# Gate and up of 18 feed-forward tiles as a 2x2 block product with seven block products instead of eight

## The chip, the cores and the metric

The kernel runs on one core of a Trainium2 chip, as one launch. The metric is the device time of that core in microseconds. Three runs of the kernel before gave 1388.51, 1388.89 and 1391.63 us; the median is 1388.89 us. TensorE does the matrix products (PE in the profile, PEld its weight loads), VectorE (DVE) and ScalarE (ACT) the element-wise work, GpSimd (POOL) a little more of it and some DMA issues, and SyncE (SP) issues most DMAs.

## The reference

Two layers of a recurrent decoder. Each has a mixer and a SwiGLU feed-forward, both modulated by shift, scale and gate vectors computed from a condition, and both followed by a layer norm. 512 prompt tokens and 8 sample tokens go through the same weights. What the change touches:

```python
D_MODEL = 1024; DEPTH = 2; D_FF = 2816      # D_FF: 22 tiles of 128 columns

def swiglu(h, w_in, w_out):
    gate, up = jnp.split(jnp.einsum('bld,df->blf', h, w_in), 2, axis=-1)
    return jnp.einsum('blf,fd->bld', jax.nn.silu(gate) * up, w_out)

for l in range(DEPTH):
    mod = jnp.einsum('bd,de->be', silu(c), w_ada[l]) + b_ada[l]      # 6 x D_MODEL columns
    sh_m, sc_m, gt_m, sh_f, sc_f, gt_f = jnp.split(mod, 6, axis=-1)
    out = mixer_l(x * (1 + sc_m) + sh_m)                             # even, then odd (S5 and HGRN2)
    x = layer_norm(ALPHA * x + (1 + gt_m) * out, ln_g[l, 0], ln_b[l, 0])
    h = x * (1 + sc_f) + sh_f
    x = layer_norm(ALPHA * x + (1 + gt_f) * swiglu(h, ffn_w_in[l], ffn_w_out[l]), ln_g[l, 1], ln_b[l, 1])
```

All inputs are float32.

## The kernel before

Activations lie features on partitions, tokens along the free axis: 8 blocks (`k`) of 128 features, and 520 tokens as two halves (`hf`) of `HN` = 260. An activation is kept as two float32r parts, `hhi` and `hlo` (the rounded value and the rest), and so is each weight (`whi`, `wlo`); a product is the three matmuls hi·hi, lo·hi and hi·lo. So one tile of 128 output columns is 8 blocks x 2 halves x 3 = 48 matmuls of 128x128 weights and 260 columns. This is `mm3` (lines 231 to 241).

Weights come through `WS` (lines 152 to 226), a stream in the order of the list `plan`. `load` issues one DMA into one of three `raw` tiles; `make` turns 128 columns of it into a pair: `S.copy` on ACT rounds to `whi` (L199), `sub` on DVE leaves the rest in `wlo` (L110). Three such pairs exist (pool `whl`), used in turn. `take` makes the pair of this unit and of the next at raised priority. Where `first_units` runs, two pairs go to another pool, tag `W` (`wxh`, `wxl`).

`ffn` (from line 835) does the 22 tiles of gate and up in two halves of 11, with the down projection of each half behind it. Gate goes to SiLU (ACT), up is multiplied with it (DVE, L110 `sg<-acc,sg`), and the product is split into `ah` (ACT) and `al` (DVE). PSUM has two `acc` tiles of two banks and four `mx` tiles of one bank. At the start of a feed-forward `first_units` does the first five units (a unit is gate or up of one tile) for the first token half and then for the second, because the layer norm delivers the halves one after the other. The last feed-forward (`l` = 1) is the last stage of the kernel.

The modulation vectors (`ada`) are matmuls with 32 columns of weights, four side by side in the array, over chunks of 1 MB that are mixed into `plan`: 10 blocks of 1024 outputs, 4 chunks each (L323). In the S5 preparation, 32 groups get a small 128x16 product each (`pM`, L1620), done while the first feed-forward runs.

The order of instructions on each engine is fixed when the program is built, by a scheduler that goes by data dependences, buffers and priorities; on the chip each engine takes its queue in that order and waits at semaphores.

Of the kernel before, what the change touches and what calls it, by code (L numbers as in the profile page):

```python
# [34 lines left out]
FIRST = 3000  # L35
EV_COLS = [256, 1552, 512, 1808, 768, 1024, 1280, 2064, 2320]
# [3 lines left out]
def build(tc, I, O):  # L40
    nc = tc.nc
    V, S, G, T, SY = nc.vector, nc.scalar, nc.gpsimd, nc.tensor, nc.sync
    with ExitStack() as ctx:
# [107 lines left out]

        class WS:
# [29 lines left out]
            def make(self, u):  # L182
# [6 lines left out]
                if kind in ("ada", "lr"):  # L189
                    self.prep[u] = r  # L190
                    return
                m = min(128, ncol)
# [8 lines left out]
                self.prep[u] = (hi, lo)  # L201

# [10 lines left out]
            def ada(self):  # L213
                while self.i < len(units) and plan[units[self.i][0]][0] == "ada":
# [4 lines left out]
                    if p_[2] == 6:  # L219
                        ada_rows(self.acc, p_[6], p_[4] // 128)  # L220
# [27 lines left out]
        def p_ada(l, js):  # L248
            return [("ada", I["w_ada"][l], k0, 2, D * j, D, l) for j in js for k0 in range(0, 8, 2)]
# [4 lines left out]
        def p_ffn(l, hb):  # L254
            r = []
            for c in range(0, 11, 2):
                n = min(2, 11 - c) * 128
                c0 = (11 * hb + c) * 128
                r.append(("fin", f_in[l], 0, 8, c0, n))
# [16 lines left out]

        FA = p_ada(0, [5]) + p_ada(1, [0])
        FB = p_ada(1, [1, 2])
        OA = p_ada(1, [3, 4])
        LA = p_ada(1, [5])  # L280
        plan.append(("lr", ev_in, 0, 8, 1536, 16))
        plan += p_cols("in", ev_in, [0])
        plan += mix(p_cols("in", ev_in, EV_COLS), p_ada(0, range(2, 4)))
        plan += mix(p_cols("out", ev_out, (0, 256)), p_ada(0, [4])[:2], 1) + p_ada(0, [4])[2:] + p_cols("out", ev_out, (512, 768))
# [5 lines left out]
        plan += mix(p_ffn(1, 0)[:12], LA, 2, 1) + p_ffn(1, 0)[12:] + p_ffn(1, 1)  # L290
# [18 lines left out]
        def ada_mm(p, r):  # L309
# [4 lines left out]
            sb = cst.tile([128, 256], F32, tag="adasb", name="adasb")  # L314
# [5 lines left out]
        def ada_part(p, k0, r):  # L320
            for k in range(2):
                for c in range(4):
                    T.matmul(p[32 * c:32 * c + 32, 0:256], condT[:, k0 + k, :], r[:, k, 256 * c:256 * c + 256],  # L323
                             start=(k0 + k == 0), stop=(k0 + k == 7), tile_position=(0, 32 * c), skip_group_check=True)

        def ada_rows(p, l, j):
            sb = cst.tile([128, 256], F32, tag="adasb", name="adasb")
            S.copy(sb, p[:, 0:256])
            for b in range(2):
                transpose(p[:, 256 + 128 * b:384 + 128 * b], sb[:, 128 * b:128 * b + 128])  # L330
# [1687 lines left out]
```

## Time and profile before

| | |
|---|---|
| median of three runs | 1388.89 us |
| profiled execution, its own time | 1391.37 us |
| span of the profile | 1389.4 us |
| PE busy in the span | 1333.4 us, 96% |
| DVE, ACT, POOL busy | 55%, 36%, 14% |
| mean granted TensorE clock | 0.985 of full speed |
| last feed-forward | about 994 to 1389 us of the span |

The profile is one execution. Times in its rows are microseconds from the start of the span unless they are marked ns. PE's busy time counts the time in which a matmul is under way; since matmuls are pipelined, one lasts longer than the distance to the next. Busy shares are averages over stages with different limits, so a stage is read by its own rows.

### The profile page before, as it was taken

How to read it: one execution, taken by the hardware profiler on the slowest of the kernel's cores; microseconds unless marked ns; L12 is line 12 of the kernel's file. 1: busy time of each engine (PE TensorE's matmuls, PEld its weight loads, DVE VectorE, ACT ScalarE, POOL GpSimd, SP SyncE). 2: the span in 40 equal slices, each digit the busy share in tenths (PEclk: the TensorE clock that was granted, in tenths of full speed). 3: DMA queues.
4: the chain of work that ended last, by engine and by line, in shares of the span. 5: the costliest groups of instructions: out<-in, count | busy, mean ns of one | idle time of the engine just before them, and what ended most of it. 6: DMA issues, size and time to landing. Idle time of an engine off the chain costs nothing. (4 is left out here: it accounts for less than half of the span.)

```text
span 1389.4 us, 29467 instructions
## 1 busy us (share of the span) xinstructions
PE 1333.4 (96%) x12687; PEld 1267.0 (91%) x12687; DVE 764.9 (55%) x1726; ACT 498.2 (36%) x802; POOL 191.8 (14%) x215
## 2 busy tenths in 40 slices
PE   6998999989999999999998999999999999999996
PEld 4797988989998999999988999889899999999996
DVE  4677755687997233233592785566833233232365
ACT  3555536353232222222264123363533222222231
POOL 2200010340011200000170421013500000000013
PEclk9999999999999999999999999999999999999998
DMA  9643363413345842444458446432333323221211
GB/s 277 197 152 101 91 212 120 154 48 120 116 166 205 234 152 92 152 133 158 150 200 169 131 147 216 126 126 92 101 113 107 118 95 122 92 92 54 84 62 63
DMA packets 157628, 185.53 MB, mean 134 GB/s; under 512 B 18188, under 2 KB 137354, under 8 KB 157242
## 3 DMA queue, kind: packets, MB, share of 16 engines
q1 hardware_dynamic: 151514, 166.43, 38.7%
q0 software_dynamic: 5744, 17.08, 3.8%
q8 instruction: 100, 1.64, 0.5%
q14 instruction: 30, 0.25, 0.1%
q10 hardware_dynamic: 240, 0.13, 0.0%
HBM read 167.11 MB, written 15.36 MB: 131 GB/s over the span
## 5 line engine op out<-in xcount | busy, mean ns | idle before, releaser
L237 PE MATMUL acc<-hhi,whi 128*128 128x260 f32 x1936 | 398.8, 287 | 3.0 <-ACT whi L199 1.3
L199 ACT CAST whi<-raw 128x1024 fp32r<-128x1024 f32 (+2 forms) x198 | 187.7, 955 | 587.1 <-PE acc L239 428.1
L239 PE MATMUL acc<-hlo,whi 128*128 128x260 f32 x1936 | 396.2, 286 | 1.2 <-DVE hlo L110 1.2
L241 PE MATMUL acc<-hhi,wlo 128*128 128x260 f32 x1936 | 395.1, 285 | 0.0
L110 DVE TENSOR_TENSOR wlo<-raw,whi 128x1024 fp32r<-128x1024 f32 (+2 forms) x198 | 220.2, 1116 | 222.3 <-ACT whi L199 220.7
L237 PEld LDWEIGHTS acc<-hhi,whi 128*128 128x128 f32 x1936 | 300.5, 190 | 16.1 <-issue 5.9
L239 PEld LDWEIGHTS acc<-hlo,whi 128*128 128x128 f32 x1936 | 300.6, 190 | 4.4 <-DVE hlo L110 1.7
L241 PEld LDWEIGHTS acc<-hhi,wlo 128*128 128x128 f32 x1936 | 300.9, 190 | 2.3 <-issue 1.7
L239 PE MATMUL acc<-al,whi 128*128 128x260 f32 x576 | 116.0, 283 | 2.3 <-DVE al L110 2.3
L237 PE MATMUL acc<-ah,whi 128*128 128x260 f32 x576 | 116.4, 284 | 1.4 <-DVE x L122 0.8
L241 PE MATMUL acc<-ah,wlo 128*128 128x260 f32 x576 | 115.7, 283 | 0.0
L110 DVE TENSOR_TENSOR sg<-acc,sg 128x520 f32<-128x520 f32 (+1 forms) x48 | 31.0, 653 | 112.6 <-PE acc L241 108.1
L237 PEld LDWEIGHTS acc<-ah,whi 128*128 128x128 f32 x576 | 88.3, 188 | 4.8 <-ACT whi L199 2.3
L239 PEld LDWEIGHTS acc<-al,whi 128*128 128x128 f32 x576 | 88.6, 188 | 2.5 <-DVE al L110 2.5
L241 PEld LDWEIGHTS acc<-ah,wlo 128*128 128x128 f32 x576 | 88.6, 188 | 0.0
L524 POOL TENSOR_TENSOR s<-x 128x520 f32<-128x520 f32 x4 | 6.9, 1720 | 568.1 <-ACT whi L199 321.6
L110 DVE TENSOR_TENSOR smp<-acc,gt 128x8 f32<-128x8 f32 (+1 forms) x72 | 11.6, 161 | 119.0 <-PE acc L241 94.5
L816 PE MATMUL acc<-hhi,whi 128*128 128x260 f32 x208 | 59.2, 287 | 3.3 <-ACT hhi L774 3.3
L818 PE MATMUL acc<-hlo,whi 128*128 128x260 f32 x208 | 58.8, 289 | 3.3 <-DVE hlo L767 1.9
L817 PE MATMUL acc<-hhi,wlo 128*128 128x260 f32 x208 | 58.3, 282 | 0.0
L122 DVE SCALAR_TENSOR_TENSOR x<-acc,gt,x 128x512 f32<-128x512 f32 (+1 forms) x72 | 44.8, 622 | 0.0
L323 PE MATMUL mx<-raw,condT 128*32 128x256 f32 x640 | 44.2, 384 | 0.0
(592 smaller groups left out, 2017.5 us busy)
## 6 DMA issues: line engine op xcount, KB each, us to landing
raw<-in_w_ada_dram SPq DMA_DIRECT2D x40, 1024.0 KB, 6.1
raw<-in_ffn_w_in_dram SPq DMA_DIRECT2D x40, 1024.0 KB, 5.2
raw<-in_ffn_w_out_dram SPq DMA_DIRECT2D x16, 1024.0 KB, 5.3
raw<-in_ev_w_in_dram SPq DMA_DIRECT2D x10, 1024.0 KB, 9.4
raw<-in_od_w_in_dram SPq DMA_DIRECT2D x10, 1024.0 KB, 5.9
raw<-in_w_ada_dram SPq DMA_DIRECT2D x16, 512.0 KB, 7.3
raw<-in_ffn_w_out_dram SPq DMA_DIRECT2D x16, 384.0 KB, 3.1
raw<-in_ev_w_out_dram SPq DMA_DIRECT2D x4, 1024.0 KB, 5.3
```

The source lines that it names most:

```text
L110: V.tensor_tensor(out=out, in0=a, in1=b, op=op)
L122: V.scalar_tensor_tensor(out=out, in0=a, scalar=s, in1=b, op0=op0, op1=op1)
L199: S.copy(hi[:, :nk, :m], rj)
L237: T.matmul(acc[:, hf, :HN], wh[:, k - koff, :], ah(k)[:, hf, :], start=st, stop=False)
L239: T.matmul(acc[:, hf, :HN], wh[:, k - koff, :], al(k)[:, hf, :], start=False, stop=False)
L241: T.matmul(acc[:, hf, :HN], wl[:, k - koff, :], ah(k)[:, hf, :], start=False, stop=sp)
L323: T.matmul(p[32 * c:32 * c + 32, 0:256], condT[:, k0 + k, :], r[:, k, 256 * c:256 * c + 256], start=(k0 + k == 0), stop=(k0 + k == 7), til ...
L524: G.tensor_tensor(out=lnt["s1"], in0=x[:, 0] if m == 1 else lnt["s1"], in1=x[:, m], op=ALU.add)
L816: T.matmul(out, wh[:, k, :], ah(k)[:, hf, :], start=n == 0, stop=False)
L817: T.matmul(out, wl[:, k, :], ah(k)[:, hf, :], start=False, stop=False)
L818: T.matmul(out, wh[:, k, :], al(k)[:, hf, :], start=False, stop=n == len(ks) - 1)
```

## The change

Seen per tile f, gate and up form a 2x2 block matrix: rows gate and up, columns the lower and the upper four feature blocks. The activation forms another: rows the lower and the upper four feature blocks, columns the two token halves. The kernel before computes the eight block products. The changed one computes seven, by a scheme with sums of blocks ahead of and behind the products (each block product is 4 feature blocks x 3 = 12 matmuls). It does so for tiles 4 to 21 of the last feed-forward. Tiles 0 to 3 stay as they were.

`t_forms` makes the sums of activation blocks once, on DVE and ACT: `t1`, `t2`, `t4`, and `t3` in place of a block of `hhi`/`hlo` that is no longer needed. `sw_weights` makes four pairs per tile, in four steps: w1 (both gate blocks), w2 (one up block), wu and wg (two sums each, formed in place in `raw`). `sw_unit` runs the seven products, and forms the sums behind them by copies and additions in PSUM.

Beside that: the modulation matmuls take 512 columns at a time instead of 256 (half as many instructions, 5 blocks of 2048 outputs), and the four chunks that lay in the last feed-forward move to the first layer's input projection. The small S5 product swaps its operands: `CS` (32 columns of two groups) becomes the weights, four side by side, and two transposes per 8 groups put the result back. The pool of the final layer norm's tiles opens behind the tiles of `t_forms`. Some small tiles change place.

```diff
+SW0 = 4
+        def sw_weights(r, w, walloc):
+            g, u = r[:, 0], r[:, 1]
+
+            def parts(t, src, hs):
+                for q in hs:
+                    S.copy(t[0][:, q], src[:, q])
+                    sub(t[1][:, q], src[:, q], t[0][:, q].bitcast(F32))
+
+            def pair():
+                return tuple(whl.tile([128, 8, 128], F32R, tag=nm, name=nm) for nm in ("whi", "wlo"))
+
+            w.append(pair())
+            parts(w[0], g, (LO, UP))
+            yield
+            w.append(pair())
+            parts(w[1], u, (UP,))
+            add(u[:, UP], u[:, LO], u[:, UP])
+            sub(u[:, LO], g[:, LO], u[:, LO])
+            sub(g[:, LO], u[:, UP], g[:, LO])
+            sub(g[:, UP], g[:, UP], g[:, LO])
+            yield
+            w.append(walloc())
+            parts(w[2], u, (UP, LO))
+            yield
+            w.append(walloc())
+            parts(w[3], g, (LO, UP))
...
+                if kind == "sw":
+                    w = self.prep[u] = []
+                    self.gen = sw_weights(r, w, self.walloc)
+                    for _ in range(1 if plan[units[u - 1][0]][0] == "sw" else 4):
+                        next(self.gen, None)
+                    return
...
-            return [("ada", I["w_ada"][l], k0, 2, D * j, D, l) for j in js for k0 in range(0, 8, 2)]
+            return [("ada", I["w_ada"][l], k, 1, D * j, 2 * D, l) for j in js for k in range(8)]
...
-        plan += mix(p_ffn(1, 0)[:12], LA, 2, 1) + p_ffn(1, 0)[12:] + p_ffn(1, 1)
+        plan += p_ffn(1, 0) + p_ffn(1, 1)
...
-                             start=(k0 + k == 0), stop=(k0 + k == 7), tile_position=(0, 32 * c), skip_group_check=True)
+                T.matmul(p[32 * c:32 * c + 32, 0:512], condT[:, k, :], r[:, 0, 512 * c:512 * c + 512],
+                         start=(k == 0), stop=(k == 7), tile_position=(0, 32 * c), skip_group_check=True)
...
+                    for lo, up in qs:
+                        q1, q2, q3 = t2k("q1"), t2k("q2"), t2k("q3")
+                        join(q3, lo, 1)
+                        join(q1, lo, 0)
+                        sub(q1, q3, q1)
+                        parts(t1, lo, q1)
+                        join(q2, up, 1)
+                        sub(q2, q2, q1)
+                        parts(t2, lo, q2)
+                        join(q3, up, 0)
+                        sub(q3, q3, q2)
+                        parts(t4, lo, q3)
+                    for lo, up in qs:
+                        q2, q3 = t2k("q2"), t2k("q3")
+                        join(q3, lo, 1)
+                        join(q2, up, 1)
+                        sub(q2, q2, q3)
+                        parts(t3, lo, q2)
...
+                def sw_unit(f):
+                    w1, w2, wu, wg = ws.get("sw", 128 * f)
+                    t1, t2, t3, t4, b11, b21, b22 = tf
+                    o1, o2, e = acc_tile(), acc_tile(), mx()[:, :HN]
+                    a_, d_, c_, b_ = o1[:, 0, :HN], o1[:, 1, :HN], o2[:, 0, :HN], o2[:, 1, :HN]
+
+                    def prod(out, w, off, t, st):
+                        for k in range(4):
+                            T.matmul(out, w[0][:, off + k], t[0][:, k], start=st and k == 0, stop=False, skip_group_check=True)
+                            T.matmul(out, w[1][:, off + k], t[0][:, k], start=False, stop=False, skip_group_check=True)
+                            T.matmul(out, w[0][:, off + k], t[1][:, k], start=False, stop=k == 3, skip_group_check=True)
+
+                    soon = lambda: tc.high_priority(offset=HIGH)
+                    prod(a_, w1, 0, b11, True)
+                    with soon():
+                        S.copy(b_, a_)
+                    prod(e, wu, 4, t1, True)
+                    p5 = t2k("p5")[:, 0]
+                    with soon():
+                        S.copy(p5, e)
+                    prod(b_, wg, 0, t2, False)
+                    with soon():
+                        add(d_, b_, p5)
+                    prod(a_, w1, 4, b21, False)
+                    ws.more()
+                    prod(b_, wu, 0, t3, False)
+                    ws.more()
+                    with soon():
+                        S.copy(c_, b_)
+                    prod(d_, wg, 4, b22, False)
+                    ws.more()
+                    prod(c_, w2, 4, t4, False)
+                    with soon():
+                        add(b_, b_, p5)
+                    m = f % 11
+                    fin_ev(0, m, 0, o1[:, :, :HN])
+                    fin_ev(1, m, 0, o2[:, :, :HN])
...
-                        T.matmul(pM[:, g * 16:(g + 1) * 16], BA[:, g].rearrange("p e h -> p (e h)"), CS[:, gg],
-                                 start=True, stop=True)
+                        T.matmul(pM[32 * c:32 * c + 32, 128 * (g // 4):128 * (g // 4) + 128],
+                                 CS[:, gg:gg + 2].rearrange("p a b -> p (a b)"), BA[:, g].rearrange("p e h -> p (e h)"),
+                                 start=g < 4, stop=True, tile_position=(0, 32 * c), skip_group_check=True)
```

The order on VectorE in the last feed-forward, in the kernel before, over two tiles (`wlo` is a weight's rest, `sg` the product with the gate, `al` its rest):

```order
L110 TENSOR_TENSOR al_11640<-sg_12408,ah_11639 128x520
L110 TENSOR_TENSOR sg_12464<-acc_12529,sg_12464 128x520
L110 TENSOR_TENSOR wlo_12692<-raw_12585,whi_12691 128x1024
L110 TENSOR_TENSOR al_11640<-sg_12464,ah_11639 128x520
L110 TENSOR_TENSOR wlo_12706<-raw_12585,whi_12705 128x1024
L110 TENSOR_TENSOR wlo_12764<-raw_12695,whi_12763 128x1024
L110 TENSOR_TENSOR sg_12636<-acc_12711,sg_12636 128x520
L110 TENSOR_TENSOR wlo_12874<-raw_12819,whi_12873 128x1024
```

The same engine in the changed kernel, over one tile (7) in the first half; raw_12205 holds the weights of tile 8, raw_12333 those of tile 9. `acc_12336<-acc_12337,p5` is the sum behind product 3, `wlo_12392` is w2, `wxl_12412` is wu, `wlo_12456` is w1, `wxl_12431` is wg:

```order
L111 TENSOR_TENSOR acc_12336<-acc_12337,p5_12364 128x260
L111 TENSOR_TENSOR wlo_12392<-raw_12205,whi_12391 128x512
L111 TENSOR_TENSOR raw_12205<-raw_12205 128x512 x2
L111 TENSOR_TENSOR wxl_12412<-raw_12205,wxh_12411 128x512
L111 TENSOR_TENSOR raw_12205<-raw_12205 128x512
L111 TENSOR_TENSOR acc_12337<-acc_12337,p5_12364 128x260
L111 TENSOR_TENSOR raw_12205<-raw_12205 128x512
L111 TENSOR_TENSOR sg_12449<-acc_12337,sg_12449 128x520
L111 TENSOR_TENSOR wxl_12412<-raw_12205,wxh_12411 128x512
L111 TENSOR_TENSOR wlo_12456<-raw_12333,whi_12455 128x512 x2
L111 TENSOR_TENSOR wxl_12431<-raw_12205,wxh_12430 128x512 x2
L111 TENSOR_TENSOR al_11528<-sg_12449,ah_11527 128x520
```

Where one tile had 2 rests of 1024 columns, one product and one split, it now has 7 rests and 4 sums of 512 columns, 2 sums of 260, one product and one split: 15 instructions. wg, which product 3 of tile 8 reads, stands behind all but the last of them.

VectorE in the changed kernel where tile 4, the first of the new form, begins; `sg_11876` is the product of the last old unit, raw_11553 holds tile 4's weights, `q1`, `q2`, `q3` are sums of activation blocks, `t1l` is the second half of t1's rest, and `wlo_12072` is w1 of tile 5:

```order
L111 TENSOR_TENSOR sg_11876<-acc_11964,sg_11876 128x520
L111 TENSOR_TENSOR q3_12058<-hhi_85,hlo_86 128x520
L111 TENSOR_TENSOR wxl_11953<-raw_11553,wxh_11952 128x512
L111 TENSOR_TENSOR wlo_12072<-raw_11883,whi_12071 128x512 x2
L111 TENSOR_TENSOR q2_12057<-hhi_85,hlo_86 128x520
L111 TENSOR_TENSOR q2_12042<-q2_12042,q1_12041 128x520
L111 TENSOR_TENSOR q3_12043<-hhi_85,hlo_86 128x520
L111 TENSOR_TENSOR raw_11553<-raw_11553 128x512
L111 TENSOR_TENSOR t1l_12020<-q1_12041,t1h_12019 128x520
L111 TENSOR_TENSOR wxl_11953<-raw_11553,wxh_11952 128x512
L111 TENSOR_TENSOR al_11528<-sg_11876,ah_11527 128x520
L111 TENSOR_TENSOR q2_12057<-q2_12057,q3_12058 128x520
```

`t1l`, which product 2 of tile 4 reads, stands nine instructions behind the product of the last old unit, and the sums that belong to t2, t3 and t4 are still to come.

## Rows read from the trace of the kernel before

**Rows 1.** The page, part 1: busy us (share of the span) xinstructions.
```profile
PE 1333.4 (96%) x12687; PEld 1267.0 (91%) x12687; DVE 764.9 (55%) x1726; ACT 498.2 (36%) x802; POOL 191.8 (14%) x215
```
**Rows 2.** Busy time by stretches: length, then PE, PEld, DVE, ACT, POOL, PEclk, DMA, GB/s.
```profile
392.00:440.00 48.00, 45.15 (x396) 43.67 (x394) 40.80 (x42) 14.25 (x24) 5.95 (x9) 1.00 0.55 189
...
1052.00:1166.00 114.00, 114.00 (x971) 111.98 (x971) 37.25 (x56) 30.86 (x42) 0.00 (x0) 1.00 0.34 109
1166.00:1260.00 94.00, 94.00 (x785) 94.00 (x784) 30.39 (x35) 24.47 (x31) 0.00 (x0) 1.00 0.30 96
```
**Rows 3.** VectorE in order of time, last feed-forward: start, duration, [idle before <-releaser].
```profile
1263.16 0.70 DVE L110 TENSOR_TENSOR sg<-acc,sg 128x520 f32<-128x520 f32 x1 [3.65 <-PE acc L241]
...
1268.93 0.70 DVE L110 TENSOR_TENSOR sg<-acc,sg 128x520 f32<-128x520 f32 x1 [3.08 <-PE acc L241]
```
**Rows 4.** VectorE from 900 us, by shape: xcount | busy us, mean ns | idle before.
```profile
L110 DVE TENSOR_TENSOR sg<-acc,sg 128x520 f32<-128x520 f32 x20 | 14.0, 700 | 68.7 <-PE acc L241 68.7
...
L110 DVE TENSOR_TENSOR sg<-acc,sg 128x260 f32<-128x260 f32 x4 | 1.5, 420 | 2.7 <-PE acc L818 2.7
...
L110 DVE TENSOR_TENSOR wlo<-raw,whi 128x512 fp32r<-128x512 f32 x2 | 1.4, 690 | 0.0
```
**Rows 5.** VectorE in order of time, pairs that stand directly behind each other.
```profile
993.25 0.41 DVE L110 TENSOR_TENSOR x<-x,rs 128x256 f32<-128x256 f32 x1
993.58 0.41 DVE L767 TENSOR_TENSOR hlo<-h32h,hhi 128x256 fp32r<-128x256 f32 x1
...
1009.53 1.22 DVE L110 TENSOR_TENSOR wlo<-raw,whi 128x1024 fp32r<-128x1024 f32 x1
1010.66 0.76 DVE L110 TENSOR_TENSOR al<-sg,ah 128x260 fp32r<-128x260 f32 x2
```
**Rows 6.** ScalarE from 900 us, by shape.
```profile
L78 ACT ACTIVATE sg<-acc 128x520 f32<-128x520 f32 x19 | 11.3, 597 | 0.0
...
L741 ACT COPY mu<-mx 128x260 f32<-128x260 f32 x2 | 0.7, 370 | 0.5 <-PE mx L700 0.5
L199 ACT CAST whi<-raw 128x512 fp32r<-128x512 f32 x1 | 0.6, 617 | 4.0 <-PE acc L239 4.0
```
**Rows 7.** All engines in order of time: a weight buffer's last reader, and the cast into it.
```profile
1022.49 0.40 PE L239 MATMUL acc<-hlo,whi 128*128 128x260 f32 x2
...
1022.99 1.05 ACT L199 CAST whi<-raw 128x1024 fp32r<-128x1024 f32 x1 [3.51 <-PE acc L239]
...
1024.07 1.23 DVE L110 TENSOR_TENSOR wlo<-raw,whi 128x1024 fp32r<-128x1024 f32 x1 [0.20 <-ACT whi L199]
```
**Rows 8.** TensorE in order of time around one modulation chunk.
```profile
1051.56 0.40 PE L241 MATMUL acc<-hhi,wlo 128*128 128x260 f32 x2
1051.89 1.07 PE L323 MATMUL mx<-raw,condT 128*32 128x256 f32 x16
1052.89 0.50 PE L237 MATMUL acc<-hhi,whi 128*128 128x260 f32 x2
```
**Rows 9.** TensorE over the whole span, by line.
```profile
L323 PE MATMUL mx<-raw,condT 128*32 128x256 f32 x640 | 44.2, 384 | 0.0
...
L1620 PE MATMUL mx<-CS,BA 128*128 128x16 f32 x64 | 7.4, 257 | 0.0
...
L147 PE MATMUL mx<-ident,BA 128*128 128x128 f32 x32 | 4.1, 272 | 0.0
```
**Rows 10.** The DMA issues, the page's part 6.
```profile
raw<-in_ffn_w_in_dram SPq DMA_DIRECT2D x8, 512.0 KB, 4.1
```
**Rows 11.** TensorE in order of time: the longest wait for data in mid-kernel.
```profile
765.98 3.18 PE L1716 MATMUL mx<-u,bt 128*64 128x72 f32 x48 [5.94 <-DMA u<-Usd]
```
**Rows 12.** TensorE alone, three stretches of 3 us around it (busy, PEclk, DMA, GB/s).
```profile
764.00:767.00 3.00, 1.02 (x17) 0.61 1.09 284
767.00:770.00 3.00, 3.00 (x40) 0.50 0.53 152
770.00:773.00 3.00, 3.00 (x22) 0.75 0.19 64
```

More of the change, by code (lines that the diff above doesn't have):

```diff
@@ L174, in load @@
                     t = wraw.tile([128, 2048], F32, tag="raw", name="raw")
+                    if kind == "sw":
+                        v = t.rearrange("p (g k c) -> p g k c", g=2, k=8)
+                        for g in range(2):
+                            SY.dma_start(v[:, g], src[:, DFF * g + c0:DFF * g + c0 + 128].rearrange("(k p) c -> p k c", p=128))
+                        self.raw[self.dma] = v
+                        self.dma += 1
+                        continue
                     v = t[:, :nk * ncol].rearrange("p (k c) -> p k c", k=nk)
@@ L201, in make, with more @@
                 self.prep[u] = (hi, lo)
+            def more(self):
+                with tc.high_priority(offset=self.off):
+                    next(self.gen, None)
             def take(self):
@@ L258, in p_ffn @@
                 c0 = (11 * hb + c) * 128
+                if l and 11 * hb + c >= SW0:
+                    r += [("sw", f_in[l], 0, 8, c0 + 128 * j, 128) for j in range(n // 128)]
+                    continue
                 r.append(("fin", f_in[l], 0, 8, c0, n))
@@ L275, in mix @@
             return r
[L277 to L280, printed above, removed]
+        E2, E4 = p_ada(0, [2]), p_ada(0, [4])
+        FA, FB, OA = p_ada(1, [0]), p_ada(1, [2]), p_ada(1, [4])
         plan.append(("lr", ev_in, 0, 8, 1536, 16))
         plan += p_cols("in", ev_in, [0])
-        plan += mix(p_cols("in", ev_in, EV_COLS), p_ada(0, range(2, 4)))
-        plan += mix(p_cols("out", ev_out, (0, 256)), p_ada(0, [4])[:2], 1) + p_ada(0, [4])[2:] + p_cols("out", ev_out, (512, 768))
+        plan += mix(p_cols("in", ev_in, EV_COLS), E2 + E4[:4])
+        plan += mix(p_cols("out", ev_out, (0, 256)), E4[4:6], 1) + E4[6:] + p_cols("out", ev_out, (512, 768))
         plan += mix(p_ffn(0, 0)[:12], FA[:4], 3) + mix(p_ffn(0, 0)[12:], FA[4:])
@@ L848, in ffn @@
                     for d in range(0, 11, 2):
+                        if l and f0 + d >= SW0:
+                            break
                         nj = min(2, 11 - d)
@@ L882, in ffn @@
                             next(side, None)
+                    if l:
+                        if hb == 0:
+                            with tc.high_priority(offset=200):
+                                tf[:] = t_forms()
+                        for f in range(max(SW0, f0), f0 + 11):
+                            sw_unit(f)
+                        if hb:
+                            swx.close()
                     for _ in side or ():
@@ L899, in ffn @@
                 prep = ln_prep(l, 1, (1, 0, 1)) if l == 0 else None
-                final = None if l == 0 else final_tools(fp)
+                final = None if l == 0 else final_tools(swx.enter_context(tc.tile_pool(name="fin", bufs=1, reuse_waits="tile")))
                 for m in range(4, 8):
```

61 lines of the change are left out of this document (42 added, 19 removed).

## The prediction

> **What bounds the kernel now.** First the page's busy shares: PE is busy 96% of the span, DVE 55%, ACT 36% [rows 1]. A share over the whole span hides stages, so next the stretches of the last feed-forward: PE is busy all of the time from 1052 to 1260 us at full clock, DVE for a third of it [rows 2]. The reader is to see that this stage is matmuls and nothing else, and that two thirds of VectorE stand free. Then the price of a unit: two up units in a row end 5.77 us apart [rows 3], which is 48 matmuls, so 0.1202 us each. Last the prices on VectorE and ScalarE, since the change pays there: durations by shape [rows 4, 6], and how far apart two instructions start [rows 5], because a queue moves by that distance, not by the duration.
>
> **The matmuls saved.** A tile had 2 x 48 = 96 matmuls and gets 7 x 12 = 84. Eighteen tiles save 216, times 0.1202 us: 26.0 us. A product of 12 takes 1.44 us, a tile 10.10 instead of 11.54.
>
> **What VectorE pays.** Starts lie 0.33 us apart for 256 columns and 1.13 for 1024 [rows 5]; on the line between, 0.60 us for 512, 0.34 for 260, 0.61 for 520. A tile had two rests of 1024, one product and one split: 2 x 1.13 + 2 x 0.61 = 3.5 us. It gets eleven instructions of 512, two of 260, two of 520: 6.6 + 0.68 + 1.22 = 8.5 us of the tile's 10.10. That fits as a sum. It need not fit in time, because most of these instructions can't start early, and that is where I think the gain goes.
>
> Follow the buffers. Three pairs serve w1 and w2 in turn: w2 of tile f+1 gets the pair that w1 of tile f leaves, and w1 is last read by product 4. Only then does ScalarE cast w2's block, VectorE takes its rest, and only then may the sums be formed in place in raw, for the first overwrites that block. wu and wg of tile f+1 come out of these sums, and product 3 of tile f+1 reads wg. So one chain runs from the end of product 4 of a tile to product 3 of the next:
> - the cast into a freed pair starts 0.10 us behind the modelled end of its last reader, 0.26 us behind the place where the next matmul starts [rows 7];
> - cast of 512 columns 0.62 us [rows 6], hand-over 0.03 [rows 7];
> - w2's rest 0.69 in full [rows 4] and 0.03, because the next reads what it frees;
> - two sums 1.20, a wait of about 0.17 for ScalarE's cast of wu, wu's first rest 0.60, a sum 0.60, wu's second rest 0.60, the PSUM sum 0.34, a sum 0.60, both rests of w1 for the tile behind 1.20, the product with the gate 0.61, wg's first rest in full 0.69, hand-over 0.03: 6.64.
>
> Together 0.26 + 0.65 + 0.72 + 6.64 = 8.27 us. TensorE has products 5, 6, 7, 1, 2 and one matmul in between: 5 x 1.44 + 0.12 = 7.33. So product 3 of each tile waits 0.94 us. The order is a little different in the second half (w1 ahead of the product), with the same sum. Tile 11 doesn't pay it, as its weights are made beside the down projection, nor do tile 4, which has its own bill, and tile 5, whose weights are made while tile 4 stands. Fifteen tiles pay: 14.1 us. VectorE is the engine that decides here: if its distance is a twentieth off, the chain moves by 0.33 us a tile, 5 us in all. Nearer than that the rows don't bound it, since none shows such a chain.
>
> **The start at tile 4.** The activation sums are 28 instructions of 520 columns on VectorE (12 joins, 8 differences and 8 rests; I count all as 0.61). Most stand behind instructions that wait for TensorE: the product with the gate of tile 2 waits for the second-last old unit and so can't start before 5.55 us ahead of the last one's end. From it to t1's last rest VectorE's new order has 21 instructions: -5.55 + 20 x 0.605 + 0.7 puts its end 7.3 us behind the start of tile 4. Product 2 wants it 6 matmuls in, at 1.44 + 0.72 = 2.16: a wait of 5.1. Eight more instructions (4.8 us) lead to wg's first rest, at 12.1; product 3 wants it at 7.3 + 0.72 + 0.12 = 8.1: 4.0. Seven more end t3's second half at about 16.4, which product 5 wants at 15.5: about 1.0. Together 10.1 us, once. Nothing hides it, since TensorE's queue has only tile 4 next. In the second half there is no such bill.
>
> **The small edits.** The modulation: a chunk of 16 matmuls takes 1.0 us in four rounds of four [rows 8], 40 chunks in all (640 matmuls [rows 9]). Now 8 of twice the columns in two rounds: the same columns, two changes of round fewer. From nothing to 0.1 us a chunk, 0 to 4 us; I take 1.5, since columns fill most of a round. Four chunks leave the last feed-forward, where TensorE is never idle, and enter the first input projection, where it is nearly so: 0, give or take 1. The S5 product: 64 matmuls cost 7.4 us, 0.116 each for 16 columns [rows 9]. Per 8 groups there come 16 matmuls of 128 columns, four side by side, about half of a modulation chunk [rows 8], 0.55 us, and two transposes of 0.13 [rows 9]: 0.8 instead of 1.85, 4.2 in all. In this stretch VectorE is busy 40.8 of 48 us and PE already idle 2.85 [rows 2], so some comes back as waits: 0 to 4.2, I take 3.5. A weight load of 512 KB in rows of 128 columns lands in 4.1 us [rows 10]; two per tile are 8.2 of a tile's 11 and are issued more than a tile ahead: 0. The final layer norm's tiles wait for tile 21, some 60 us ahead of use: 0.
>
> **The sum.** -26.0 + 14.1 + 10.1 - 1.5 - 3.5 = -6.8 us, on the profiled execution's 1391.4 us (span 1389.4 and 2.0 around it). That execution lies 2.5 above the median of the runs, 1388.9; from the median the sum gives 1382 us.
>
> **Rivals.** (a) VectorE keeps up: the chain is shorter than I think, by 0.6 us of its 8.27, and the start costs 8 because ScalarE and VectorE run ahead more. Then -26.0 + 15 x 0.34 + 8 - 5 = -18: 1371 us. For it: VectorE's free time [rows 2]. Against: the buffer order, which no free time shortens.
>
> (b) Slower than before: VectorE's queue moves by full durations, 0.69 for 512 [rows 4], as soon as each instruction reads what one just ahead wrote or freed. The eleven distances in the chain grow by 0.09, so product 3 waits 1.9 us; the start's 29 grow too, to 12.6. -26.0 + 15 x 1.9 + 12.6 - 5 = +10: 1399 us. It decides from a distance of 0.64 us on, where the waits eat the 26.0 and the small edits. Against it: the pairs in rows 5 are apart less than they last, by 0.08 and 0.09. [...]
>
> [...]
>
> (d) The change doesn't do what it says: its order has 84 matmuls a tile for all eighteen, so this has no chance of its own.
>
> **How the numbers follow.** The forecast has 0.5, its own range 1376 to 1389 (chain 0.6 to 1.2 us a tile, small edits 1 to 8); (a) 0.15, (b) 0.15, (c) 0.2. About 0.3%, 4.2 us, is what a measurement of this kernel can tell from no change: faster means under 1384.7, slower over 1393.1. Faster: 0.35 of the forecast's 0.5, all of (a), 0.06 of (c): 0.56. Slower: 0.14 of (b) and 0.03 of the rest: 0.17. Between: 0.27. The range for 8 in 10 takes in most of (a) and half of (b): 1368 to 1395.
>
> **What would show it.** In the profile after: 84 matmuls a tile and tiles about 11.0 us apart, with PE idle about 0.9 us ahead of product 3, released by wg's rest on VectorE (or by the copy into PSUM beside it), in fifteen tiles; VectorE over 80% busy in the tiles; about 10 us of idle PE in tile 4, in products 2 and 3; L1620's successor at under half of 7.4 us. I am wrong in the main if tiles are 10.1 us apart (then the chain isn't there) or over 11.6, if product 3 waits for something else than VectorE or ScalarE, or if tile 4 starts without a gap.

## The result and the profile after

| kernel | median, us | ratio to before, 95% interval |
|---|---|---|
| before | 1389.4 | |
| changed | 1414.2 (1412.0 to 1415.6) | 1.0175 [1.0155, 1.0195] |
| predicted | 1382 (1368 to 1395) | |

The change costs 24.8 us; the forecast was a gain of 6.8. The profiled execution took 1415.4 us, span 1413.3, mean granted clock 0.974. Three executions that were hundreds of microseconds longer than all others of their kernel (one each of `fill`, `half2_v4` and the kernel before) are left out of all medians and ratios.

The page, part 1, of the changed kernel answers [rows 1]:
```profile
PE 1323.4 (94%) x12159; PEld 1237.9 (88%) x12159; DVE 875.0 (62%) x1947; ACT 555.9 (39%) x957; POOL 192.7 (14%) x215
```
There are 528 matmuls fewer, PE's busy time is down by 10 us, and the span is up by 24. So TensorE waits. The distance of tiles is read as in [rows 3], from VectorE's products with the gate, in order of time (start, duration); there is one a block tile:
```profile
1037.09 0.69 DVE L111 TENSOR_TENSOR sg<-acc,sg 128x520 f32<-128x520 f32 x1
...
1061.42 0.69 DVE L111 TENSOR_TENSOR sg<-acc,sg 128x520 f32<-128x520 f32 x1
...
1072.27 0.69 DVE L111 TENSOR_TENSOR sg<-acc,sg 128x520 f32<-128x520 f32 x1
...
1096.93 0.69 DVE L111 TENSOR_TENSOR sg<-acc,sg 128x520 f32<-128x520 f32 x1
...
1109.30 0.69 DVE L111 TENSOR_TENSOR sg<-acc,sg 128x520 f32<-128x520 f32 x1
...
1221.34 0.69 DVE L111 TENSOR_TENSOR sg<-acc,sg 128x520 f32<-128x520 f32 x1
...
1233.36 0.69 DVE L111 TENSOR_TENSOR sg<-acc,sg 128x520 f32<-128x520 f32 x1
```
The first block tile ends 24.3 us after the last plain one, the second 10.85 us behind it. From there tiles of the first half are 12.3 to 12.4 us apart (the last 11.3), of the second half 12.02. Plain tiles were 11.54 apart, and the forecast was 11.04. What TensorE waited for from 1000 to 1360 us (engine, line, releaser: us in total, times, longest), the four longest in total:
```profile
PE acc L939 <- DVE acc L111: 10.1, 18, 0.6
PE acc L939 <- ACT acc L946: 7.6, 10, 0.8
PE acc L940 <- DVE wxl L111: 7.4, 6, 3.4
PE mx L941 <- DVE t1l L111: 3.1, 1, 3.1
```
The reader is to see the first row: a wait in every one of the 18 tiles that the prediction does not have. One tile of the first half, all engines in order of time:
```profile
1110.71 0.37 ACT L946 COPY acc<-acc 128x260 f32<-128x260 f32 x1
...
1111.71 1.28 DVE L111 TENSOR_TENSOR wxl<-raw,wxh 128x512 fp32r<-128x512 f32 x2
...
1112.45 0.39 PE L940 MATMUL acc<-t2h,wxl 128*128 128x260 f32 x1 [0.92 <-DVE wxl L111]
...
1114.15 0.44 DVE L111 TENSOR_TENSOR acc<-acc,p 128x260 f32<-128x260 f32 x1 [0.54 <-PE acc L941]
...
1114.64 0.39 PE L939 MATMUL acc<-hhi,whi 128*128 128x260 f32 x1 [0.60 <-DVE acc L111]
```
Product 3 (t2h) waits for wg's rest, as predicted, 0.92 us. Product 4 (hhi, whi) then stands still until VectorE has written `d_ = b_ + p5`. It does not read d_: it adds to a_, the other bank of the same tile. And each wait costs more than its idle time: the three starts around the first lie 1.4 us beyond the usual 0.12, the two at the second 0.87, since idle time is counted from the modelled end of a matmul and the first two matmuls behind a wait stand 0.2 us apart. In the second half the trace names another releaser of product 3, ScalarE's copy (L946), but wg's rest stands right beside it. All engines in order of time:
```profile
1221.94 1.28 DVE L111 TENSOR_TENSOR wxl<-raw,wxh 128x512 fp32r<-128x512 f32 x2
...
1222.47 0.39 PE L939 MATMUL acc<-t2h,wxh 128*128 128x260 f32 x1 [0.77 <-ACT acc L946]
```
The first of these two rests ends at about 1222.63, and the second matmul of product 3, which reads it, starts at 1222.70. The copy had ended at 1222.42.

The start, TensorE in order of time, matmuls behind a wait:
```profile
1039.04 0.39 PE L940 MATMUL mx<-t1h,wxl 128*128 128x260 f32 x1 [1.36 <-DVE wxl L111]
...
1043.29 0.58 PE L941 MATMUL mx<-t1l,wxh 128*128 128x260 f32 x1 [3.14 <-DVE t1l L111]
...
1048.15 0.58 PE L940 MATMUL acc<-t2h,wxl 128*128 128x260 f32 x1 [3.41 <-DVE wxl L111]
...
1051.54 0.59 PE L939 MATMUL acc<-hhi,whi 128*128 128x260 f32 x1 [0.64 <-DVE acc L111]
```
and stretches of 3 us (PE, PEld, DVE, ACT, POOL busy, then PEclk), as in [rows 12]:
```profile
1041.00:1044.00 3.00, 0.71 (x3) 0.71 (x4) 3.00 (x6) 1.24 (x2) 0.00 (x0) 0.50 0.00 0
...
1053.00:1056.00 3.00, 3.00 (x15) 3.00 (x15) 0.77 (x2) 0.62 (x1) 0.00 (x0) 0.50 0.85 254
1056.00:1059.00 3.00, 3.00 (x21) 3.00 (x20) 2.77 (x5) 1.42 (x4) 0.00 (x0) 0.72 0.00 0
```
Products 2 and 3 wait, as the prediction said, 7.9 us of idle time for its 9.1; the 0.64 at product 4 is the wait that it does not have, and its 1.0 at product 5 did not come. VectorE is busy without a break beside the first three (6 instructions in each 3 us until 1050 us), and the granted clock is at 0.50 of full speed from 1041 to 1056 us.

The rows that answer to [rows 9], TensorE over the whole span, by shape:
```profile
L370 PE MATMUL mx<-raw,condT 128*32 128x512 f32 x320 | 41.9, 604 | 1.9 <-DMA raw<-in_w_ada_dram 1.9
...
L1755 PE MATMUL mx<-BA,CS 128*32 128x128 f32 x64 | 2.6, 279 | 0.0
...
L148 PE MATMUL mx<-ident,mt 128*128 128x128 f32 x8 | 1.5, 271 | 0.0
```
The small edits did on TensorE about what was priced: 44.2 became 41.9, and 7.4 became 2.6 and 1.5. But L370 now waits 1.9 us for the DMA of a chunk, where the row of before has 0.0.

### The profile page after: what moved, and what is told of

It is laid out like the page before. It is cut to its first block, busy times and chain, and to the rows that moved or that the text cites. A ratio compares the mean times of both kernels' runs of the same rounds, so it can differ in the third digit from the quotient of the medians.

```text
span 1413.3 us, 28868 instructions
## 1 busy us (share of the span) xinstructions
PE 1323.4 (94%) x12159; PEld 1237.9 (88%) x12159; DVE 875.0 (62%) x1947; ACT 555.9 (39%) x957; POOL 192.7 (14%) x215
## 5 line engine op out<-in xcount | busy, mean ns | idle before, releaser
L111 DVE TENSOR_TENSOR wlo<-raw,whi 128x1024 fp32r<-128x1024 f32 (+2 forms) x216 | 212.2, 993 | 179.5 <-ACT whi L242 133.6
L242 ACT CAST whi<-raw 128x1024 fp32r<-128x1024 f32 (+2 forms) x162 | 149.9, 933 | 419.6 <-PE acc L286 284.7
L284 PE MATMUL acc<-hhi,whi 128*128 128x260 f32 x1360 | 283.4, 289 | 2.7 <-ACT whi L242 1.3
L286 PE MATMUL acc<-hlo,whi 128*128 128x260 f32 x1360 | 282.6, 288 | 0.9 <-DVE hlo L111 0.9
L288 PE MATMUL acc<-hhi,wlo 128*128 128x260 f32 x1360 | 278.3, 285 | 0.0
L284 PEld LDWEIGHTS acc<-hhi,whi 128*128 128x128 f32 x1360 | 211.6, 190 | 22.9 <-issue 9.6
L286 PEld LDWEIGHTS acc<-hlo,whi 128*128 128x128 f32 x1360 | 212.4, 190 | 5.3 <-issue 2.1
L288 PEld LDWEIGHTS acc<-hhi,wlo 128*128 128x128 f32 x1360 | 211.8, 190 | 2.0 <-issue 1.3
L111 DVE TENSOR_TENSOR smp<-acc,gt 128x8 f32<-128x8 f32 (+1 forms) x72 | 11.6, 161 | 117.6 <-PE acc L288 91.7
L863 PE MATMUL acc<-hhi,whi 128*128 128x260 f32 x208 | 59.9, 289 | 3.3 <-ACT hhi L821 3.3
L111 DVE TENSOR_TENSOR wxl<-raw,wxh 128x512 fp32r<-128x512 f32 (+1 forms) x82 | 62.1, 771 | 1.2 <-ACT wxh L242 1.0
L160 ACT CAST whi<-raw 128x512 fp32r<-128x512 f32 x54 | 31.7, 620 | 78.8 <-issue 50.7
L865 PE MATMUL acc<-hlo,whi 128*128 128x260 f32 x208 | 59.0, 291 | 3.2 <-DVE hlo L814 1.8
L864 PE MATMUL acc<-hhi,wlo 128*128 128x260 f32 x208 | 59.0, 286 | 0.0
L939 PE MATMUL acc<-hhi,whi 128*128 128x260 f32 x144 | 43.2, 300 | 10.1 <-DVE acc L111 10.1
```

Source lines behind the costliest of these rows:

```text
L111: V.tensor_tensor(out=out, in0=a, in1=b, op=op)
L160: S.copy(t[0][:, q], src[:, q])
L242: S.copy(hi[:, :nk, :m], rj)
L284: T.matmul(acc[:, hf, :HN], wh[:, k - koff, :], ah(k)[:, hf, :], start=st, stop=False)
L286: T.matmul(acc[:, hf, :HN], wh[:, k - koff, :], al(k)[:, hf, :], start=False, stop=False)
L288: T.matmul(acc[:, hf, :HN], wl[:, k - koff, :], ah(k)[:, hf, :], start=False, stop=sp)
```

## The experiments

Theory: the block product loses by three things of the order of work and of buffers, each of which can be taken away alone: the late activation sums at the start, product 4's wait for a bank that it doesn't touch, and product 3's wait. Rivals: the early edits; VectorE's load as such (a wait taken away comes back at the next product); the clock. Medians are of each run's own set, and ratios are to the runs of before on the same chip. The sets' runs of before had medians from 1389.4 to 1391.1 us, so a difference between medians of two sets is good to 1 or 2 us; the ratios are free of this.

| run | median, us | ratio, 95% interval |
|---|---|---|
| no_blocks | 1393.7 | 1.0025 [1.0013, 1.0037] |
| nb_olds5 | 1395.1 | 1.0028 [1.0011, 1.0045] |
| own_bank | 1403.8 | 1.0090 [1.0075, 1.0105] |
| p4_first | 1410.4 | 1.0152 [1.0105, 1.0199] |
| early2 | 1404.5 | 1.0097 [1.0072, 1.0122] |
| fill | 1411.7 | 1.0136 [1.0101, 1.0171] |
| v4be2 | 1392.6 | 1.0007 [0.9990, 1.0024] |
| half2_v4 | 1392.8 | 1.0018 [1.0000, 1.0037] |
| obe2 | 1389.5 | 0.9987 [0.9971, 1.0003] |
| lean | 1392.5 | 1.0014 [0.9998, 1.0030] |
| v6p | 1399.1 | 1.0063 [1.0043, 1.0084] |
| obe3 | 1371.2 | 0.9865 [0.9832, 0.9898] |

**no_blocks**
```
-SW0 = 4
+SW0 = 22      # and no activation sums
```


> The changed kernel with all 22 tiles of the last feed-forward as plain products again; the new modulation chunks, their new places and the turned S5 product stay. Theory: the loss lies in the block tiles. In the changed kernel's trace everything ahead of the last feed-forward ended 5.9 us later, of which 4 moved modulation chunks are about 4.4, and these 4.4 then leave the last feed-forward; so this run ends about 1.5 us over the kernel before, at 1391 us (1387 to 1395). Rival: the edits ahead of the last feed-forward are a loss of their own of 6 us or more; then about 1396 us or over.

1393.7 us, 2.9 over its runs of before, between the two expectations and nearer to the theory's 1.5. The block tiles thus cost 20.5 of the loss; the early edits are a small loss where I had forecast a gain of 5. TensorE's wait for a chunk (L370) is here too, 2.0 us.

**own_bank**
```
-a_, d_, c_, b_ = o1[:, 0, :HN], o1[:, 1, :HN], ...
+a_, d_, c_, b_ = o1[:, 0, :HN], e, ...
-fin_ev(0, m, 0, o1[:, :, :HN])
+fin_ev(0, m, 0, o1[:, 0:1, :HN], slice(0, 1))
+fin_ev(0, m, 0, e.unsqueeze(1), slice(1, 2))
...
```


> The changed kernel with the sum b + p5 written into the bank of product 2 and no longer into the second bank of the tile into which product 4 accumulates; the SiLU then runs in two halves. Nothing that product 4 needs comes from VectorE then. Theory: product 4 waits only because both banks belong to one tile; 0.76 us of distance for each of 17 or 18 tiles goes, 13 us, and ScalarE's extra 0.2 us a tile is beside it: 1401 us (1398 to 1404). Rival: VectorE's queue is the bound of a tile, and the wait moves on to product 5 or to the next product 3: 1414 us, within 2.

10.4 us less, and product 4's wait is gone from the list of TensorE's waits: it was for the tile, not for the data. Tiles of the second half, VectorE in order of time:
```profile
1213.56 0.69 DVE L111 TENSOR_TENSOR sg<-acc,sg 128x520 f32<-128x520 f32 x1
...
1224.88 0.69 DVE L111 TENSOR_TENSOR sg<-acc,sg 128x520 f32<-128x520 f32 x1
```
They are 11.32 apart for 12.02, so 0.7 of the wait's 0.8 went there; product 3's wait grew from 0.77 to 1.00 us of idle time. That the gain is short of 13 goes with this: product 3's waits, 11.6 us behind the first block tile in the changed kernel (7.6 for the copy, 4.0 for wg's rest), are 18.0 now and all for the copy (TensorE's waits, 1000 to 1360 us):
```profile
PE acc L939 <- ACT acc L946: 18.0, 17, 1.7
```
The change's two banks were guarded as one tile: product 4, which touches only one of them, stood still until VectorE had written the other, 18 times (10.1 us of idle time in the changed kernel), and that is what went.

**p4_first**
```
+prod(a_, w1, 4, b21, False)
 prod(b_, wg, 0, t2, False)
 with soon():
     add(d_, b_, p5)
-prod(a_, w1, 4, b21, False)
```


> The changed kernel with product 4 ahead of product 3; nothing else. Theory: product 3 has 1.47 us more until its weights are wanted, and the second weight pair comes free 1.47 us earlier, so product 3's wait (1.1 to 1.4 us a tile) goes; product 5 now stands right behind product 3 and must wait for the sum that reads its bank, 0.6 to 0.8 us a tile as product 4 did. Some 18 to 20 us less, 1395 us (1390 to 1402). Rival: VectorE's queue is the bound of a tile (9.0 us of 12.3 busy, with waits between): then the period stays at 12 us or over and the time at 1414 us, within 3.

Only some 4 us less; the intervals of the two ratios overlap, and neither expectation holds. The trace is of the slowest of its four executions (1421.2 us). The weights' wait did go behind the first block tile, and the expected wait of product 5 came, but a second that I had not expected came with it, TensorE in order of time:
```profile
1223.28 0.39 PE L939 MATMUL acc<-hhi,wxh 128*128 128x260 f32 x1 [0.53 <-DVE acc L111]
...
1231.27 0.39 PE L939 MATMUL acc<-hhi,whi 128*128 128x260 f32 x1 [0.45 <-ACT acc L946]
```
Product 4 adds to the bank that the copy of product 1 reads, and now stands too close behind. A tile of the second half takes 11.68 us. Its first block tile took 27.3 us. The waits were moved, not removed.

**early2**
```
 first_units(...)
+if l:
+    forms = t_forms()      # t1, t2, t4; yields ahead of t3
+    next(forms)
 for u in fins[n0:]:
```


> The changed kernel with the sums of the activations (t1, t2, t4) formed right behind the first five plain tiles' halves, not at the end of the plain tiles; only t3, which overwrites an operand of the plain tiles, stays where it was. Theory: the 25 us that the first block tile took (12.3 a tile later on) come from VectorE's backlog of 21 us at that place, 18 sums of the activations among it, and from the clock that fell to 0.50 behind the waits; 8 to 12 us less, 1404 us (1401 to 1408). Rival: the first tile's own weights, whose four parts are made at one go, set its waits, and the clock falls as before: at most 3 us less, 1411 to 1414 us.

9.7 us less. The last plain unit and the first block tile, VectorE in order of time:
```profile
1037.31 0.69 DVE L111 TENSOR_TENSOR sg<-acc,sg 128x520 f32<-128x520 f32 x1
...
1049.66 0.69 DVE L111 TENSOR_TENSOR sg<-acc,sg 128x520 f32<-128x520 f32 x1
```
Two stretches of 3 us in that tile (PE, PEld, DVE, ACT, POOL busy, then PEclk):
```profile
1041.00:1044.00 3.00, 2.40 (x20) 2.19 (x19) 1.05 (x3) 0.00 (x0) 0.00 (x0) 1.00 0.38 110
1044.00:1047.00 3.00, 3.00 (x27) 3.00 (x27) 1.88 (x3) 1.48 (x3) 0.00 (x0) 1.00 0.80 240
```
The tile takes 12.35 us for 24.3, like any other: the start is gone, and the clock (1.00) doesn't fall. The next tile takes 12.38 for 10.85, so of the 12 us some 10.4 stay.

**fill**
```
 T.matmul(e, wu[0][:, 4 + k], t1[0][:, k], ...)
+if k == 0: filler(12, wu[0][:, 4], t1[0][:, 0])
 T.matmul(e, wu[1][:, 4 + k], t1[0][:, k], ...)
+if k == 2: filler(27, wu[0][:, 6], t1[0][:, 2])
 ...
+filler(30, wg[0][:, 0], t2[0][:, 0])
```


> The changed kernel with 68 further matmuls in the first block tile, in the places where TensorE waited there (38 behind the first matmul of product 2, 30 ahead of product 3); they write a bank that nobody reads, and the waits of the other instructions stay as they are. They are 8.2 us of work in the 8.5 us that TensorE stood still. Theory: behind those waits the granted clock was 0.50 for some 15 us, and from the first rest of product 3's weights (1048.15) to the end of the tile the 59 matmuls and a wait of 0.6 us took 13.3 us where 7.7 would do at full clock; with the clock held up 5 us go: 1409 us (1407 to 1411). Rival: VectorE's queue alone sets the end of that tile, and the clock costs nothing beside it: 1414 us, within 2, or as much later as the further matmuls are late.

There were 69 of them. Inconclusive: the median is 2.5 us lower and the ratio points to 5, but its interval overlaps that of the changed kernel. The trace shows no gain: the first two block tiles took 35.35 us (1036.06 to 1071.41) for 35.18 in the changed kernel, the first of them 23.6. The clock held through the filled waits (1.00 until 1050 us) and fell behind the next one:
```profile
1047.00:1050.00 3.00, 1.57 (x11) 1.37 (x11) 3.00 (x6) 0.00 (x0) 0.00 (x0) 1.00 0.03 5
1050.00:1053.00 3.00, 2.48 (x13) 2.48 (x14) 1.16 (x3) 0.63 (x1) 0.00 (x0) 0.67 0.78 229
1053.00:1056.00 3.00, 3.00 (x21) 3.00 (x20) 2.13 (x4) 0.65 (x2) 0.00 (x0) 0.76 0.40 120
```
VectorE is still busy without a break until 1050 us, which fits the rival that it sets the end. What the clock alone costs there stays open.

**nb_olds5**
```
 (no_blocks, and)
-T.matmul(pM[32*c:...], CS[:, gg:gg+2]..., BA[:, g]..., tile_position=(0, 32*c))
+T.matmul(pM[:, g*16:(g+1)*16], BA[:, g]..., CS[:, gg])
...
```


> The run without block tiles (1393.7 us), with the S5 product as it was before (64 matmuls of 16 columns and one copy for every 8, no transposes). Theory of the prediction: the turned product is worth 3.5 us; the copies of the matrix took 44.5 us from first to last in the changed kernel and 46.5 before, so at least 2 of it are seen; then this run is 2 to 3.5 us slower, 1396 to 1397 us. Rival: the two further transposes and their copies give back what the matmuls save, and it is at 1393.7, within 1. If the turned product is a loss, it is below 1392.

1.4 us over no_blocks, with ratios that can't be told apart. That the 3.3 us that TensorE saves reach the end is not seen; the two intervals leave room for some of it. The small loss of no_blocks is then left to the modulation chunks and the order of the early projections. L370's wait for a chunk's DMA, 2.2 us here too and 0.0 before, is of about its size; none of this was tried alone.

**obe2** (own_bank and early2)

> The changed kernel with two repairs together: the sum b + p5 in a bank of its own (own_bank) and the sums of the activations formed early (early2). Theory: product 4's wait and the start are losses apart from each other, so both gains stand: 1414.2 - 10.4 - 9.7 = 1394 us (1391 to 1397), and what is left in a tile is product 3's wait alone. Rival: they are in part one thing (VectorE's queue), and the sum is short by half of the smaller: 1399 us or over.

1389.5 us, 24.7 less than the changed kernel and 4.6 better than the sum of the two, so outside the expected range to the good; why is not shown. No difference from the kernel before can be told. What is left is one wait a tile. All engines in order of time:
```profile
1210.77 0.68 DVE L111 TENSOR_TENSOR wxl<-raw,wxh 128x512 fp32r<-128x512 f32 x1
...
1212.60 0.69 DVE L111 TENSOR_TENSOR sg<-acc,sg 128x520 f32<-128x520 f32 x1
...
1213.33 0.36 ACT L947 COPY acc<-acc 128x260 f32<-128x260 f32 x1
...
1213.74 0.39 PE L940 MATMUL acc<-t2h,wxh 128*128 128x260 f32 x1 [1.00 <-ACT acc L947]
```
Product 3 waits for the copy of product 1 into b_, and the copy starts 0.04 us after VectorE's product of the tile before has ended: that one still reads the buffer, because a block tile takes both buffers of the pool. It is not the weights here: the rest of wg that product 3 reads (first line) had ended 2.3 us ahead of product 3, and 1.3 ahead of where the wait began.

**lean** (obe2 without the four sums of weight blocks, so its products are not the layer's)
```
 (obe2, and)
-add(u[:, UP], u[:, LO], u[:, UP])
-sub(u[:, LO], g[:, LO], u[:, LO])
-sub(g[:, LO], u[:, UP], g[:, LO])
-sub(g[:, UP], g[:, UP], g[:, LO])
```


> As obe2, with the four in-place sums and differences of the weight blocks on VectorE left out (2.9 us a tile), so products 2, 3, 5 and 6 work on other weights than they should; every matmul, cast, rest and transfer stays. Theory: product 3's wait (1.1 to 1.4 us a tile in the changed kernel) hangs on VectorE's chain of sums and rests between the end of product 4 and the rest of wg; without 2.9 us of it the wait goes, 1375 us (1371 to 1382). Rival: the wait hangs on when the weight buffers come free and on the casts; then the period stays over 11 us and the time within 4 us of obe2.

1392.5 us, no gain at all. TensorE still waits for the copy:
```profile
1235.46 0.39 PE L936 MATMUL acc<-t2h,wxh 128*128 128x260 f32 x1 [1.06 <-ACT acc L943]
```
The rest of wg that product 3 reads ended at 1231.35, 4.1 us ahead. So the wait that was left is neither VectorE's load nor the weight chain on which the prediction had built.

**obe3**
```
 (obe2, and)
-o1, o2, e = acc_tile(), acc_tile(), mx()[:, :HN]
+o2, a_, e = acc_tile(), mx()[:, :HN], mx()[:, :HN]
```


> As obe2, with the first product's sum in a bank of its own too, so that the tile of the two banks c and b is all that a block tile takes of its pool, and the pool's second buffer serves the next block tile. Theory: in obe2 product 3 waits 1.0 us a tile for ScalarE's copy of product 1 into bank b, and that copy waits for VectorE's multiplication of the tile before, which still reads the one buffer there is; the rest of wg, which product 3 waited for in the changed kernel, was in some 1.2 us earlier than product 3 was due there. With the second buffer the wait goes (1.1 us of distance, 17 tiles), a tile is 10.1 to 10.4 us, and the time 1389.5 - 19 = 1371 us (1367 to 1377). Rival: the rest of wg becomes the next wait at once, since VectorE's queue is no shorter, and a tile stays at 11 us or over: 1386 us or more.

1371.2 us: 18.3 less than obe2, 1.35% [1.02, 1.68] less than the kernel before. VectorE in order of time:
```profile
1069.93 0.70 DVE L111 TENSOR_TENSOR sg<-acc,sg 128x520 f32<-128x520 f32 x1
...
1080.04 0.70 DVE L111 TENSOR_TENSOR sg<-acc,sg 128x520 f32<-128x520 f32 x1
...
1225.35 0.70 DVE L111 TENSOR_TENSOR sg<-acc,sg 128x520 f32<-128x520 f32 x1
...
1235.64 0.70 DVE L111 TENSOR_TENSOR sg<-acc,sg 128x520 f32<-128x520 f32 x1
```
and all that TensorE waited for from 1000 to 1330 us:
```profile
PE acc L284 <- DVE sg L111: 3.0, 2, 1.5
PE acc L863 <- ACT sg L79: 2.7, 1, 2.7
```
A tile takes 10.1 us, 84 matmuls and nothing else, and from the fourth block tile of the second half on 10.28: there the first starts of product 5 lie 0.22 us apart, behind VectorE's sum that reads its bank, a delay too short for the list of waits. No wait of a block product is in that list any more.

The edit also changed the order, since the scheduler goes by buffers. ScalarE in order of time, first half:
```profile
1069.39 0.62 ACT L160 CAST whi<-raw 128x512 fp32r<-128x512 f32 x1 [0.99 <-PE acc L942]
...
1070.66 0.36 ACT L947 COPY acc<-mx 128x260 f32<-128x260 f32 x1 [0.65 <-DVE sg L111]
```
The copy still waits for VectorE's product, but product 3 of the running tile is under way by then (1069.19 to 1072.10): this copy is the next tile's, 9 us ahead of its use. Products 1 and 4 of a tile now run within the tile before. And w2's cast, which followed product 4 in obe2 (at 1216.91, 0.03 us behind its end), now follows product 7 of the tile before (0.04 us behind its end), which gives the weights 11.4 us to the product 3 that reads them (1069.35 to 1080.74) instead of 7.33. So the 18.3 us are what the buffers are worth together with the order that they allow. That the copy, and not the weights, was the wait left in obe2 rests on the traces of obe2 and lean.

Three runs tried to get there by another order of products, and missed; they are told together.

**v4be2, half2_v4, v6p**
```
 products 1, 2, 4, 3, 7, 5, 6 (early2 with it)
+a_ and e in banks of their own; c_ and b_ in two acc tiles
+S.copy(cb, b_); add(c_, c_, cb)      # c_ starts with product 7
 half2_v4: SW0 = 11
 v6p: the rests of w1 on GpSimd; SiLU and product of a half as soon as it is in
```


> The changed kernel with the three repairs together, in an order of products 1, 2, 4, 3, 7, 5, 6: product 4 ahead of 3 (the weights of 3 have more time), product 7 into a bank of its own between 3 and 5 (it covers the sum that reads product 5's bank), products 1 and 4 and product 2 in banks of their own, one further sum on VectorE a tile, and the sums of the activations early as in early2. Theory: a tile is then 84 matmuls of 0.12 us and at most one short wait, 10.1 to 10.5 us; 18 tiles of 11.54 us before come to 20 to 25 us less than without block tiles (1393.7), 1371 us (1366 to 1378). Rival: VectorE, with some 9.7 us of work a tile, becomes the bound through its own order, a tile is 11 us, 1382 to 1386 us. If it is at 1394 or over, the waits named are not the cause.

> The same repaired order of products, on the 11 tiles of the second half alone; the first half's 11 tiles are plain ones. Theory: 11 tiles at 10.1 to 10.5 us for 11.54 give 11 to 16 us against 1393.7, 1380 us (1377 to 1384), so less than with 18 tiles. Rival: the tiles of the first half, where the residual's scaling stands beside them, are no gain (period 11.5 or over), and 11 tiles are as good as 18 or better.

> As v4be2 (products 1, 2, 4, 3, 7, 5, 6 with banks of their own, activations early), with two edits for VectorE's queue: the rests of the first weight pair (two of 512 columns a tile) go to GpSimd, which does nothing there, and product 7's bank is read as soon as product 5 is in, not at the tile's end. Theory: in v4be2 the tiles of the second half took 10.1 and 13.1 us in turn, because the sum that product 5 waits for stood behind three weight rests in VectorE's queue, and product 7's bank was read late; without these rests ahead of it every tile is near 10.1 to 10.6 us, 18 tiles 17 to 26 us less than plain ones: 1372 us (1367 to 1380). Rival: GpSimd's rests, 1.9 us each by a like instruction, hold VectorE up or come late for product 1, and a tile stays at 11 us or over: 1385 us or more.

None was under 1392 us. In v4be2 most tiles of the first half took 11.5 us, and those of the second 10.1 and 13.1 in turn. The waits of the long ones, TensorE in order of time:
```profile
1218.72 0.39 PE L940 MATMUL acc<-t4h,whi 128*128 128x260 f32 x1 [0.56 <-DVE sg L111]
...
1224.86 0.39 PE L940 MATMUL acc<-hhi,wxh 128*128 128x260 f32 x1 [1.54 <-DVE mx L111]
```
Product 5 waits for a sum that stood behind three weight rests in VectorE's queue; product 7 for a buffer, as in obe2. With such tiles, 11 of them are as good as 18, which was half2_v4's rival. v6p took the rests out of the queue (1.6 us each on GpSimd), but the buffer's wait grew:
```profile
1220.32 0.39 PE L940 MATMUL acc<-t4h,whi 128*128 128x260 f32 x1 [1.57 <-DVE sg L111]
```
Its tiles are 11.8 us apart on average. GpSimd's rests also held VectorE up, as the rival said. GpSimd and VectorE in order of time:
```profile
1213.26 3.31 POOL L167 TENSOR_TENSOR wlo<-raw,whi 128x512 fp32r<-128x512 f32 x2 [9.20 <-ACT whi L160]
...
1215.32 2.39 DVE L111 TENSOR_TENSOR wxl<-raw,wxh 128x512 fp32r<-128x512 f32 x2
```
Two rests of 512 columns on VectorE took 2.39 us there and 1.28 a little later, without GpSimd beside them. In the block tiles the 34 weight sums that ran beside a GpSimd rest for more than half of their time took 1.23 us on average, the 32 beside none 0.69. So v6p, 6.5 us over v4be2, doesn't tell what a shorter queue is worth. In all three runs a tile takes both buffers of the pool again. This order with one buffer a tile was not run, so what the order alone is worth stays open.

## Why the prediction was wrong

**The step that failed** is the reading of what product 4 waits for. The prediction followed the SBUF buffers of the weights and charged the PSUM sum b + p5 to VectorE alone (0.34 us in the chain). It never asked what the tile's two other banks hold up. Every product 4 waits for that sum, 18 times, 0.8 to 0.9 us each by the distance of starts, which the forecast had at nothing; taken away alone it was worth 10.4 us. A wait of PSUM buffers of the same kind, the copy into b_, was worth another 18.3 once the first and the start were gone, with the order that this allowed.

**Saved matmuls, 26.0**: right. 84 a tile, and obe3 shows 10.1 us.

**Product 3's wait, 0.94 us in fifteen tiles**: the chain and the fifteen tiles were right, the price was not. From product 4's end to the end of wg's first rest it is 8.4 us in the first half (1103.97 to 1112.39) and 8.1 in the second (1226.52 to 1234.65), for 8.27. The idle time is 0.86 to 0.93 us in four tiles, 0.41 in the last of the first half and 0.74 to 0.77 in ten of the second, where the copy ends at nearly the same time. It costs 1.1 to 1.4 us a tile. But the chain is no fixed length: w1's rests, the PSUM sum and the product with the gate, 2.15 of the 8.27, only stand ahead of wg in VectorE's queue. In obe2 they stand behind it, and the chain is 5.9 us (1216.88 to 1222.77), less than the 7.33 that TensorE has. In obe3 it no longer begins at product 4.

**The start, 10.1**: right in its two main places and near in size. 7.9 us of idle time were seen there, and the tile took 12 us more than the others; early2 gave 9.7 back.

**The clock, (c)**, which had a chance of 0.2: that it falls at the start's waits, as it did in [rows 12] behind the wait of [rows 11]. It came, 0.50 for 15 us at the start. What it costs by itself no run shows, since its share could not be told from VectorE's; with the clock at 1.00 until 1050 us (fill) the first two block tiles took as long, 35.35 us for 35.18.

**Small edits, -5.0**: wrong in sign. +2.9 in no_blocks, though the S5 product saves TensorE 3.3 us and the chunks 2.3.

**VectorE's distances**, rival (b): 0.60 us for independent instructions of 512 columns held, and the rests and sums of the chain moved at 0.60 to 0.73. The forecast's own sign of being wrong, tiles over 11.6 us apart, did come, 12.0 to 12.4, but by product 4's wait and not by these distances.

Stage by stage, by the same rows of the changed kernel and of no_blocks: the seven block tiles of the first half took 95.9 us (1037.09 to 1132.94) for 80.8 plain ones (1035.43 to 1116.24), so +15.0; from there to the last tile of the second half 194.6 for 190.2, +4.4; the rest +1.2, together the 20.6 us between the two spans. The prediction's terms gave +4.7 (-10.1 for the matmuls, 10.1 for the start, 4.7 for waits) and -6.5 (-15.9 and 9.4).

## What to carry to other kernels

When a change puts several partial sums into PSUM, list for every bank who reads it last and whether two banks that belong to one tile, or one pool with too few buffers, make an independent product wait; do this ahead of any sum of busy times. Here an arithmetic saving of an eighth per tile, 26.0 us, was lost whole to such waits and a late start; 22.5 of it (1393.7 to 1371.2) came back when the start was moved and two sums got banks of their own. Price a wait of TensorE by the distance of starts, not by the idle time that the trace prints (1.3 us against 0.92 in the first half here).

## What the runs showed beyond that

- A wait of TensorE costs more than its idle time: in the first half 0.92 us of idle time moved the next two starts by 1.3 us in sum, 0.60 by 0.87; there, at a granted clock of 1.00, the first matmul behind a wait lasts 0.39 us, the second starts 0.22 behind it, the rest 0.12.
- In the changed kernel, sums in place on VectorE (512 columns) that read what the one ahead wrote lie 0.73 us apart (two in 1.42 us, the last lasting 0.69), independent ones 0.60.
- In v6p a rest of 512 columns took 1.6 us on GpSimd (57.7 us for 36), against 0.69 on VectorE, and VectorE's sums of 512 columns beside it took 1.23 us on average for 0.69; its sums that read PSUM (128x260) did not change (0.44 for 0.43, six of them).
- In fill TensorE's granted clock held at 1.00 until 1050 us, while the 69 fillers ran, and was at 0.67 and 0.76 right after a stretch with 1.57 of 3 us busy.
